# A list scheduler's cost table is replaced: a two-layer hybrid decoder on one Trainium2 core

## The chip, the cores and the metric

The kernel runs on one core of a Trainium2 chip. Its engines are TensorE (PE, matmuls into PSUM; PEld is its loading of stationary operands), VectorE (DVE), ScalarE (ACT), GpSimd (POOL) and SyncE (SP), which here only issues loads. Each engine takes its own list of instructions in order and waits on semaphores for the others. The metric is the device time of the core in microseconds (us), from three runs and one profiled execution.

## What is computed

Two layers. Each has a half-step SwiGLU FFN, then one block in which a Mamba-2 SSD mixer and a latent-attention (MLA) mixer run side by side on the same normalised input, and then a second half-step FFN. 256 positions, model width 1024, FFN width 2816, 32 SSD heads of 64 in 4 groups with state 128, 8 attention heads, all in float32.

```python
for l in range(DEPTH):                                  # DEPTH = 2
    h = h + 0.5 * swiglu(rms_norm(h, ln_ffn1[l]), ffn1_w13[l], ffn1_w2[l])
    u = rms_norm(h, ln_mix[l])
    z, xbc, dt_raw, cq, ckv, kr, gates = split_cols(u @ w_in[l], IN_SPLIT_SIZES)
    y_ssd = ssd_branch(z, xbc, dt_raw, ...)             # conv, silu, chunked scan, norm, w_out
    y_mla = mla_branch(cq, ckv, kr, cos, sin, ...)      # q/k/v up, norms, rope, causal softmax, w_out
    g = sigmoid(gates)
    h = h + (g[..., :D_MODEL] * y_ssd + g[..., D_MODEL:] * y_mla) @ w_o[l]
    h = h + 0.5 * swiglu(rms_norm(h, ln_ffn2[l]), ffn2_w13[l], ffn2_w2[l])
```

## The kernel before

**Arithmetic.** Every large matrix product is made from split operands. A weight block of 128 x 1024 float32 is loaded by SP into a staging buffer `st` (four of them); ACT rounds it to `wh` (fp32r), DVE subtracts to get the rest, `wl` (four buffers each, `ahead`). The activations are split likewise: `X`, `oT` and `A` hold a high half of 256 columns and a low half of 256 columns (`operand`: ACT writes the high half, DVE the low one). In the FFNs, the gates and the SSD output, `mm2` makes one matmul of `wh` on both halves (512 columns) and one of `wl` on the high half (256 columns) for each 128 rows. Elsewhere `mm` makes three matmuls of 256 columns. The smaller products of the scan and of attention are in float32; the scan's output matmuls (`s<-dec,xdt`) write 64 of the 128 output rows each and come in pairs, the "narrow" form.

**Stages.** `run` goes through FFN 1, `mix`, FFN 2 for each layer. `mix` begins with the latent projections, then on DVE a chain of small steps: softplus of the time steps (tile `kn`), the latent norms (`lm`, `rly`, `rlt`, `Rc`, `Rf`), `dt`, `dA`; a small matmul on `dA` gives the cumulative sums `acum`, which go through DRAM as `rows` and come back broadcast by POOL as `row`. Then `loop_order` interleaves convolutions (`bc`, `xs`), queries, keys and values, eight `ssd` steps, eight attention `head` steps and the `z` gates. In a convolution (`conv_pair`) ACT starts `cy` and DVE adds three taps one after the other into the same tile. In `ssd`, PE transposes `xs`, DVE multiplies into `xdt`, ACT makes the decays `dec`, DVE masks them, and PE multiplies. In `head`, PE transposes queries and keys, ACT writes `qkT`, PE makes scores, DVE takes maxima, ACT exponentiates into `pp`, PE transposes that, ACT copies it to `pT`, PE makes the output. After the loop come the gates, the output projections and FFN 2.

**The order.** No engine call in the program goes to the hardware as it is written. `Queue` hands each to `Order.add`, which records it as a `Step` with its operands, works out which earlier steps it needs, and prices it with `Order.cost`: `pitch` is how long it holds its engine, `tail` what passes after that until another engine may use the result (a negative `tail` marks a load of that many bytes). `Order.arrange` then plays the program through once with these prices and writes down the order in which each engine takes its steps; `emit` issues all of them in that order, from one line (L335), so that every instruction in the profile carries it and tiles tell them apart. In `arrange`, an engine that is free looks at the first 12 (`LOOK`) of its waiting steps in program order and takes the first whose operands and buffers are ready at that time of the plan; PE wants results of other engines to be `MARGIN` older than that. SP looks only at its first step, and so keeps program order. In the plan, a result is ready for a step on the same engine after `pitch`, for another engine after `pitch + tail`. The plan's times steer nothing once the order is written: on the chip, each engine waits for what it really needs.

Of the kernel before, what the change touches and what calls it, by code (L numbers as in the profile page):

```python
# [17 lines left out]
AF = mybir.ActivationFunctionType  # L18
ALU = mybir.AluOpType

P = 128
# [16 lines left out]
XSB, ZB = 2, 1  # L38
STBUF = 4
GB, SB, HB = 4, 2, 2  # L40
LOOK, MARGIN = 12, 250.0


V_LN1, V_LNM, V_LN2 = 0, 8, 16
# [107 lines left out]


class Step:
    __slots__ = ("engine", "call", "args", "kw", "tiles", "pitch", "tail", "index", "needs", "then", "ready", "far", "at")


class Queue:
# [7 lines left out]
class Order:  # L166


    TAIL = {"PE": 190.0, "ACT": 140.0, "DVE": 120.0, "POOL": 200.0, "SP": 0.0}

    def __init__(self, nc):
        self.steps = []
        self.tensor, self.scalar = Queue(self, "PE", nc.tensor), Queue(self, "ACT", nc.scalar)
# [3 lines left out]
    @staticmethod  # L177
    def cost(engine, name, args, kw):

        views = [v for v in (*args, *kw.values()) if isinstance(v, View)]  # L180
        out = kw.get("out", args[0] if args else None)
        if name == "dma_start":
            return (600.0 if engine == "POOL" else 470.0), 4.0 * max(v.arr.size for v in views)
        size = lambda v: v.arr.size // v.shape[0]
        if engine == "PE":
            if name == "transpose":
                return 109.0, 0
            n, dt = size(kw["rhs"]), kw["lhsT"].tile.what[1]
            if dt == F32R:
                return n / 2.4 + 13.5, 0  # L190
            if dt == BF16:
                return n / 2.4 + 4.0, 0
            pair = 0.55 if out.shape[0] < P else 1.0
            return max(2 * (n / 1.2 + 2.5), 60.0) * pair, 0
        n = max(size(v) for v in views)
        if engine == "ACT":
            t = 85.0 + 0.845 * n
            if name == "activation":
                t += 45.0 * sum(isinstance(kw.get(k), View) for k in ("scale", "bias"))
                t += 235.0 * ("accum_out" in kw)  # L200
            return t, 0
        t = 66.0 + 1.042 * n
        if name == "scalar_tensor_tensor":
            t += 60.0
        return t, 0

    def add(self, engine, name, call, args, kw):
        s = Step()
        s.engine, s.call, s.args, s.kw, s.index = engine, call, args, kw, len(self.steps)
        s.pitch, size = self.cost(engine, name, args, kw)  # L210
        s.tail = self.TAIL[engine]
        if size:
            s.tail = -size
        outs = [kw["out"]] if "out" in kw else [args[0]]
        ins = [*args[0 if "out" in kw else 1:], *(v for k, v in kw.items() if k not in ("out", "accum_out"))]
        if "accum_out" in kw:
            outs.append(kw["accum_out"])
        outs = [v for v in outs if isinstance(v, View)]
        ins = [v for v in ins if isinstance(v, View)]
        before = set()  # L220
        meet = lambda a, b: a[0] < b[1] and b[0] < a[1] and a[2] < b[3] and b[2] < a[3]
        within = lambda a, b: b[0] <= a[0] and a[1] <= b[1] and b[2] <= a[2] and a[3] <= b[3]
        for v in ins:
            before.update(o for o, g in v.tile.writes if meet(g, v.region))
        for v in outs:
            t = v.tile
            before.update(o for o, g in t.writes if meet(g, v.region))
            before.update(o for o, g in t.reads if meet(g, v.region))
        for v in outs:
            t = v.tile  # L230
            t.writes = [(o, g) for o, g in t.writes if not within(g, v.region)]
            t.reads = [(o, g) for o, g in t.reads if not within(g, v.region)]
            t.writes.append((s, v.region))
        for v in ins:
            v.tile.reads.append((s, v.region))
        s.tiles = list({id(v.tile): v.tile for v in (*outs, *ins)}.values())
        for t in s.tiles:
            t.left += 1
        s.needs, s.then, s.ready, s.far, s.at = len(before), [], 0.0, 0.0, None
        for o in before:  # L240
            o.then.append(s)
        self.steps.append(s)

    def arrange(self):

        engines = ("PE", "ACT", "DVE", "POOL", "SP")
        free = dict.fromkeys(engines, 0.0)
        waiting = {e: [] for e in engines}
        wire, done = 0.0, 0
        events = []  # L250
        wake = lambda t, e: heapq.heappush(events, (t, engines.index(e)))
        for s in self.steps:
# [19 lines left out]
        while events:  # L272
            now, e = heapq.heappop(events)
# [23 lines left out]
            s = pick  # L297
            waiting[e].remove((s.index, s))
            s.at = now
            free[e] = now + s.pitch  # L300
            if s.tail < 0:
                wire = max(wire, now + 1300.0) + -s.tail / 380.0
                end = wire + (2500.0 if e == "POOL" else 700.0)
            else:
                end = now + s.pitch + s.tail
            done += 1
            wake(free[e], e)
            for t in s.tiles:
# [8 lines left out]
                    for x in engines:  # L317
                        wake(t.free_at, x)
            for n in s.then:
                near = n.engine == e and s.tail >= 0  # L320
                n.ready = max(n.ready, now + s.pitch if near else end)
                if not near:
                    n.far = max(n.far, end)
                n.needs -= 1
                if not n.needs:
                    heapq.heappush(waiting[n.engine], (n.index, n))
# [856 lines left out]
```

## Time and profile before

| | us |
|---|---|
| median of 3 runs | 1478.0 (1471.64 to 1480.55) |
| profiled execution, its own time | 1476.14 |
| its span, first to last instruction | 1474.4 |
| PE busy in the span | 1449.2 (98%) |
| DVE busy | 1148.3 (78%) |
| ACT busy | 928.4 (63%) |

The kernel's stages in the span: FFN 1 of the first layer to about 205 us, its mixer to 567, FFN 2 to 750, FFN 1 of the second layer to 932, its mixer to 1292, FFN 2 to the end. Busy time of an engine is the union of its instructions' durations; matmuls are pipelined and their ends are modelled, so how many matmuls start in a stretch says more of PE's speed than its busy time. The granted clock (PEclk) is a share of TensorE's full 2.4 GHz. A wait is idle time of an engine, put down to the instruction that ended it.

### The profile page before, as it was taken

What the parts mean: (1) busy time and instruction counts of PE and PEld (TensorE: products, weight loads), DVE (VectorE), ACT (ScalarE), POOL (GpSimd) and SP (SyncE); (2) the same over time, 40 slices, a digit from 0 to 9 for tenths busy, and PEclk for the clock granted to TensorE, in tenths of its full rate; (3) what the DMA queues carried; (4) which work ended last, traced back from release to release, by engine and by line L of the source; (5) the groups of instructions that cost most, each with busy time, mean ns of one, the idle gap of its engine ahead of it and who ended that gap; (6) DMA issues with size and microseconds to landing.
All of it is one profiled execution on the core that took longest, in us unless ns stands there. A gap on an engine that the chain in (4) does not pass through costs nothing.

```text
span 1474.4 us, 25056 instructions
## 1 busy us (share of the span) xinstructions
PE 1449.2 (98%) x9418; PEld 1309.6 (89%) x9418; DVE 1148.3 (78%) x2081; ACT 928.4 (63%) x1754; POOL 18.6 (1%) x38
## 2 busy tenths in 40 slices
PE   7999999999999999999999999989999999999999
PEld 6888898999888998888888888989999889988888
DVE  7877679889977668787677876898889676788864
ACT  6555457998875456555455554688898554565542
POOL 0000000000000000000000000000000000000000
PEclk9999999999999999999999999999999999999999
DMA  6655655455545555556655566555454455555563
GB/s 234 195 183 183 186 177 174 150 163 162 167 134 183 185 183 181 191 191 179 194 189 190 192 179 196 168 161 169 157 166 155 157 182 185 184 183 191 191 194 110
DMA packets 75978, 261.43 MB, mean 177 GB/s; under 512 B 8880, under 2 KB 11184, under 8 KB 75856
## 3 DMA queue, kind: packets, MB, share of 16 engines
q1 hardware_dynamic: 73232, 251.37, 53.1%
q0 software_dynamic: 2624, 8.46, 1.9%
q8 instruction: 74, 1.21, 0.3%
q14 instruction: 48, 0.39, 0.1%
HBM read 258.68 MB, written 1.11 MB: 176 GB/s over the span
## 4 chain that ended last, share of the span: by engine, by line
PE 81%; DVE 11%; ACT 5%; issue 2%; DMA 0%; SPq 0%; DVEq 0%; ACTq 0%
PE g L335 77%; DVE wl L335 4%; PE h L335 2%; PE s L335 2%; ACT dec L335 2%; DVE cy L335 2%; DVE dec L335 1%; ACT wh L335 1%; ACT pp L335 1%; DVE kn L335 0%; ACT A L335 0%; ACT cy L335 0%; DVE rqt L335 0%; DMA st<-in_w_dram 0%; DVE qp L335 0%
## 5 line engine op out<-in xcount | busy, mean ns | idle before, releaser
L335 DVE TENSOR_TENSOR wl<-st,wh 128x1024 fp32r<-128x1024 f32 (+2 forms) x488 | 580.7, 1192 | 239.1 <-ACT wh L335 234.8
L335 ACT CAST wh<-st 128x1024 fp32r<-128x1024 f32 (+2 forms) x488 | 499.3, 1025 | 410.3 <-PE g L335 313.7
L335 PE MATMUL g<-X,wh 128*128 128x256 f32 (+1 forms) x2464 | 617.7, 329 | 9.1 <-DVE X L335 7.0
L335 PE MATMUL g<-X,wl 128*128 128x256 f32 x1696 | 482.4, 285 | 0.0
L335 PEld LDWEIGHTS g<-X,wh 128*128 128x128 f32 x2464 | 417.8, 191 | 52.5 <-DVE X L335 7.5
L335 PE MATMUL g<-oT,wh 128*128 128x512 f32 (+1 forms) x1248 | 343.8, 344 | 0.0
L335 PE MATMUL g<-A,wh 128*128 128x512 f32 (+1 forms) x982 | 336.9, 389 | 0.0
L335 PEld LDWEIGHTS g<-X,wl 128*128 128x128 f32 x1696 | 324.7, 191 | 1.4 <-DVE wl L335 0.2
L335 PE MATMUL g<-oT,wl 128*128 128x256 f32 x976 | 274.4, 281 | 0.0
L335 PE MATMUL g<-A,wl 128*128 128x256 f32 x960 | 269.3, 281 | 0.0
L335 PEld LDWEIGHTS g<-oT,wh 128*128 128x128 f32 x1248 | 216.1, 189 | 29.6
L335 PEld LDWEIGHTS g<-A,wh 128*128 128x128 f32 x982 | 182.7, 188 | 40.0
L335 PEld LDWEIGHTS g<-oT,wl 128*128 128x128 f32 x976 | 184.9, 189 | 0.0
L335 PEld LDWEIGHTS g<-A,wl 128*128 128x128 f32 x960 | 181.5, 189 | 0.0
L335 DVE TENSOR_TENSOR t<-t,g 128x256 f32<-128x256 f32 x180 | 74.7, 415 | 0.5 <-ACT t L335 0.5
L335 DVE SCALAR_TENSOR_TENSOR cy<-g,vec,cy 128x255 f32<-128x255 f32 x144 | 68.9, 480 | 6.8 <-ACT cy L335 2.7
L335 ACT CAST A<-ta 128x256 fp32r<-128x256 f32 x88 | 35.5, 404 | 48.3 <-DVE ta L335 48.0
L335 ACT COPY t<-g 128x256 f32<-128x256 f32 x180 | 65.1, 362 | 0.3 <-PE g L335 0.3
L335 DVE TENSOR_TENSOR t<-t,Rb 128x512 f32<-128x512 f32 x88 | 60.9, 692 | 3.0
L335 PE MATMUL g<-wh,A 128*128 128x384 f32 (+1 forms) x192 | 55.4, 357 | 0.0
L335 ACT ACTIVATE dec<-row,acum 128x256 f32<-128x256 f32 (+1 forms) x128 | 49.7, 446 | 2.0 <-PE s L335 2.0
L335 ACT ACTIVATE ta<-t 128x256 f32<-128x256 f32 x88 | 36.5, 414 | 15.2 <-DVE t L335 15.1
(228 smaller groups left out, 1117.2 us busy)
## 6 DMA issues: line engine op xcount, KB each, us to landing
st<-in_w_dram SPq DMA_DIRECT2D x238, 512.0 KB, 4.2
st<-in_win_dram SPq DMA_DIRECT2D x124, 512.0 KB, 4.0
st<-in_wso_dram SPq DMA_DIRECT2D x32, 512.0 KB, 3.8
st<-in_w_dram SPq DMA_DIRECT2D x32, 384.0 KB, 3.1
row<-rows POOLq DMA_DIRECT2D x32, 256.0 KB, 3.9
st<-in_wmo_dram SPq DMA_DIRECT2D x16, 512.0 KB, 3.5
st<-in_wo_dram SPq DMA_DIRECT2D x16, 512.0 KB, 3.5
st<-in_wuq_dram SPq DMA_DIRECT2D x16, 384.0 KB, 3.6
```

Source lines behind the costliest of these rows:

```text
L335: s.call(*(take(v) for v in s.args), **{k: take(v) for k, v in s.kw.items()})
```

## The change

`Order.cost` gets a new table, and `arrange` treats some cases of their own. For ACT and DVE `tail` is now the time from a step's start to its result; `pitch` is shorter, and a dependent step on the same engine has to wait for the result too, not only for the engine (PE's own steps still follow each other after `pitch`). Prices differ by PSUM or SBUF source, by operation and by per-partition scalars. Narrow matmuls cost a switch of 95 ns in and out, functions of another activation table cost 1283 ns, PE is taken as 1.84 times slower in its first 7.5 us, the first load lands later, and `MARGIN` falls from 250 to 60 ns. 35 ns (55 ns for PE) are added to each result. No engine call of the program itself is changed.

```diff
-LOOK, MARGIN = 12, 250.0
+LOOK, MARGIN = 12, 60.0
@@ class Order
-    TAIL = {"PE": 190.0, "ACT": 140.0, "DVE": 120.0, "POOL": 200.0, "SP": 0.0}
@@ def cost
         if name == "dma_start":
-            return (600.0 if engine == "POOL" else 470.0), 4.0 * max(v.arr.size for v in views)
-        size = lambda v: v.arr.size // v.shape[0]
+            return (600.0 if engine == "POOL" else 450.0), 4.0 * max(v.arr.size for v in views)
         if engine == "PE":
             if name == "transpose":
-                return 109.0, 0
+                return 109.0, 270.0
             n, dt = size(kw["rhs"]), kw["lhsT"].tile.what[1]
             if dt == F32R:
-                return n / 2.4 + 13.5, 0
+                t = n / 2.4 + (17.0 if n > 256 else 11.0)
+                return t, t + 165.0
             if dt == BF16:
-                return n / 2.4 + 4.0, 0
-            pair = 0.55 if out.shape[0] < P else 1.0
-            return max(2 * (n / 1.2 + 2.5), 60.0) * pair, 0
+                return n / 2.4 + 4.0, n / 2.4 + 169.0
+            t = max(2 * (n / 1.2 + 2.0), 130.0)
+            if out.shape[0] < P and n > 1:
+                t = t * 0.5 + 40.0
+            return t, t + 165.0
         n = max(size(v) for v in views)
+        bank = any(v.tile.ring.bank for v in ins)
+        scalars = sum(isinstance(kw.get(k), View) for k in ("scale", "bias", "scalar", "scalar1"))
         if engine == "ACT":
-            t = 85.0 + 0.845 * n
-            if name == "activation":
-                t += 45.0 * sum(isinstance(kw.get(k), View) for k in ("scale", "bias"))
-                t += 235.0 * ("accum_out" in kw)
-            return t, 0
-        t = 66.0 + 1.042 * n
-        if name == "scalar_tensor_tensor":
-            t += 60.0
-        return t, 0
+            t = (160.0 + 0.8 * n if bank else 200.0 + 0.83 * n) + 100.0 * scalars
+            if "accum_out" in kw:
+                return t + 5.0, t + 240.0
+            return t - 100.0, t
+        slow = bank or name not in ("tensor_scalar", "tensor_copy", "memset")
+        t = 150.0 + (1.05 if slow else 0.56) * n + 60.0 * (scalars and name == "scalar_tensor_tensor")
+        return t - 83.0, t
@@ def add
-        s.tail = self.TAIL[engine]
-        if size:
-            s.tail = -size
+        s.load = name == "dma_start"
+        s.table = {AF.Silu: 1, AF.Exp: 2, AF.Tanh: 2, AF.Sin: 3}.get(kw.get("func"))
@@ def arrange
-        wire, done = 0.0, 0
+        wire, done, first, form, table = 2000.0, 0, None, False, 0
...
-            free[e] = now + s.pitch
-            if s.tail < 0:
-                wire = max(wire, now + 1300.0) + -s.tail / 380.0
-                end = wire + (2500.0 if e == "POOL" else 700.0)
-            else:
-                end = now + s.pitch + s.tail
+            pitch, tail = s.pitch, s.tail
+            if s.load:
+                wire = max(wire, now + 1300.0) + tail / 360.0
+                tail = wire + (2500.0 if e == "POOL" else 800.0) - now
+            elif e == "PE":
+                if first is None:
+                    first = now
+                if now < first + 7500.0:
+                    pitch *= 1.84
+                    tail += pitch - s.pitch
+                narrow = s.args[0].shape[0] == 64
+                if narrow != form:
+                    pitch, tail, form = pitch + 95.0, tail + 95.0, narrow
+            elif s.table and s.table != table:
+                pitch, tail, table = pitch + 1283.0, tail + 1283.0, s.table
+            free[e] = now + pitch
+            end = now + tail + 35.0
...
             for n in s.then:
-                near = n.engine == e and s.tail >= 0
-                n.ready = max(n.ready, now + s.pitch if near else end)
-                if not near:
-                    n.far = max(n.far, end)
+                if n.engine == e == "PE":
+                    n.ready = max(n.ready, free[e])
+                else:
+                    n.ready = max(n.ready, end + 20.0 * (n.engine == "PE"))
+                    n.far = max(n.far, n.ready)
```

## Rows read from the trace of the kernel before

**Rows 1.** The page's part 1: busy us, share of the span, instructions.

```profile
PE 1449.2 (98%) x9418; PEld 1309.6 (89%) x9418; DVE 1148.3 (78%) x2081; ACT 928.4 (63%) x1754; POOL 18.6 (1%) x38
```

**Rows 2.** Windows: length, busy of PE, PEld, DVE, ACT, POOL; PEclk, DMA share, GB/s.

```profile
0.00:23.00 23.00, 14.22 (x55) 11.43 (x55) 15.27 (x42) 14.36 (x28) 0.20 (x4) 0.87 0.78 261
...
205.00:430.00 225.00, 218.94 (x1667) 205.30 (x1667) 199.12 (x436) 187.86 (x428) 9.25 (x17) 0.99 0.49 158
932.00:1156.00 224.00, 217.69 (x1668) 203.86 (x1667) 197.93 (x427) 187.60 (x427) 9.13 (x17) 1.00 0.49 158
430.00:567.00 137.00, 136.80 (x920) 125.53 (x919) 95.96 (x165) 69.84 (x104) 0.00 (x0) 1.00 0.56 181
...
1292.00:1474.00 182.00, 178.83 (x1053) 158.48 (x1053) 127.56 (x190) 92.26 (x151) 0.00 (x0) 1.00 0.55 174
```

**Rows 3.** Waits of PE: total us, times, longest us.

```profile
PE g L335 <- DVE X L335: 7.0, 2, 6.7
PE s L335 <- DVE xdt L335: 4.4, 6, 1.2
PE s L335 <- DVE dth L335: 3.9, 2, 2.1
PE g L335 <- ACT wh L335: 1.8, 2, 1.0
PE h L335 <- ACT qkT L335: 1.2, 2, 0.9
PE s L335 <- DVE acum L335: 1.1, 2, 0.7
PE s L335 <- DVE BC L335: 0.8, 1, 0.8
```

**Rows 4.** Timeline of DVE, 232 to 238 us: start, duration, instruction, count.

```profile
232.60 0.55 DVE L335 RECIPROCAL kn<-kn 128x64 f32<-128x64 f32 x1
...
236.06 0.23 DVE L335 TENSOR_TENSOR Rc<-rly,rhy 128x2 f32<-128x2 f32 x2
236.33 0.16 DVE L335 TENSOR_TENSOR Rf<-Rc 128x4 f32<-128x4 f32 x1
236.53 0.17 DVE L335 TENSOR_SCALAR Rf<-Rf 128x4 f32<-128x4 f32 x1
...
236.75 1.51 DVE L335 SCALAR_TENSOR_TENSOR kn<-kn 128x64 f32<-128x64 f32 x6
```

**Rows 5.** Timeline of PE at 239 us, idle time before it in brackets.

```profile
239.03 0.83 PE L335 MATMUL s<-dA,cb 128*128 128x32 f32 x6 [2.09 <-DVE dth L335]
```

**Rows 6.** Timeline of DVE and PE, 304 to 312 us.

```profile
304.38 0.75 DVE L335 TENSOR_TENSOR xdt<-s,dth 128x256 f32<-128x256 f32 x2
...
304.86 1.52 PE L335 MATMUL s<-dec,xdt 128*64 128x256 f32 x16 [0.69 <-DVE xdt L335]
...
311.78 1.52 DVE L335 SCALAR_TENSOR_TENSOR cy<-g,vec,cy 128x255 f32<-128x255 f32 x3
```

**Rows 7.** Windows behind the first layer's stall at 239 us.

```profile
242.10:245.40 3.30, 3.30 (x18) 3.30 (x17) 2.96 (x13) 1.85 (x4) 0.13 (x1) 0.51 0.68 215
246.00:249.30 3.30, 3.30 (x30) 3.30 (x29) 3.17 (x6) 2.95 (x6) 0.72 (x2) 1.00 0.62 195
```

**Rows 8.** Windows of 150 us inside the first two FFN stages.

```profile
30.00:180.00 150.00, 150.00 (x851) 130.15 (x850) 117.92 (x201) 84.77 (x149) 0.00 (x0) 1.00 0.60 188
570.00:720.00 150.00, 150.00 (x867) 132.29 (x866) 115.94 (x178) 87.49 (x151) 0.00 (x0) 1.00 0.60 188
```

**Rows 9.** Windows in the start.

```profile
14.00:17.00 3.00, 1.21 (x6) 0.55 (x4) 2.86 (x11) 2.75 (x6) 0.00 (x0) 0.98 0.86 295
17.00:20.00 3.00, 3.00 (x11) 2.74 (x12) 2.52 (x8) 2.25 (x3) 0.00 (x0) 0.50 0.60 203
```

**Rows 10.** Groups of ACT by tile: count, busy us, mean ns, idle before.

```profile
L335 ACT ACT_TABLE_LOAD x6 | 7.7, 1283 | 0.8 <-PEq L1174 0.7
...
L335 ACT ACTIVATE sin<-ta 128x64 f32<-128x64 f32 x1 | 0.3, 256 | 0.0
```

More of the change, by code (lines that the diff above doesn't have):

```diff
@@ L154 @@
 class Step:
-    __slots__ = ("engine", "call", "args", "kw", "tiles", "pitch", "tail", "index", "needs", "then", "ready", "far", "at")
+    __slots__ = ("engine", "call", "args", "kw", "tiles", "pitch", "tail", "load", "table", "index", "needs", "then", "ready",
+                 "far", "at")
 class Queue:
@@ L181, in cost @@
         out = kw.get("out", args[0] if args else None)
+        ins = [v for v in views if v is not out]
+        size = lambda v: v.arr.size // v.shape[0]
         if name == "dma_start":
-            return (600.0 if engine == "POOL" else 470.0), 4.0 * max(v.arr.size for v in views)
-        size = lambda v: v.arr.size // v.shape[0]
+            return (600.0 if engine == "POOL" else 450.0), 4.0 * max(v.arr.size for v in views)
         if engine == "PE":
             if name == "transpose":
-                return 109.0, 0
+                return 109.0, 270.0
             n, dt = size(kw["rhs"]), kw["lhsT"].tile.what[1]
             if dt == F32R:
-                return n / 2.4 + 13.5, 0
+                t = n / 2.4 + (17.0 if n > 256 else 11.0)
+                return t, t + 165.0
             if dt == BF16:
-                return n / 2.4 + 4.0, 0
-            pair = 0.55 if out.shape[0] < P else 1.0
-            return max(2 * (n / 1.2 + 2.5), 60.0) * pair, 0
+                return n / 2.4 + 4.0, n / 2.4 + 169.0
[3 more added lines that the diff above has]
+            return t, t + 165.0
         n = max(size(v) for v in views)
+        bank = any(v.tile.ring.bank for v in ins)
+        scalars = sum(isinstance(kw.get(k), View) for k in ("scale", "bias", "scalar", "scalar1"))
         if engine == "ACT":
-            t = 85.0 + 0.845 * n
-            if name == "activation":
-                t += 45.0 * sum(isinstance(kw.get(k), View) for k in ("scale", "bias"))
-                t += 235.0 * ("accum_out" in kw)
-            return t, 0
-        t = 66.0 + 1.042 * n
-        if name == "scalar_tensor_tensor":
-            t += 60.0
-        return t, 0
+            t = (160.0 + 0.8 * n if bank else 200.0 + 0.83 * n) + 100.0 * scalars
[5 more added lines that the diff above has]
+        return t - 83.0, t
     def add(self, engine, name, call, args, kw):
@@ L209, in add @@
         s.engine, s.call, s.args, s.kw, s.index = engine, call, args, kw, len(self.steps)
-        s.pitch, size = self.cost(engine, name, args, kw)
-        s.tail = self.TAIL[engine]
-        if size:
-            s.tail = -size
+        s.pitch, s.tail = self.cost(engine, name, args, kw)
+        s.load = name == "dma_start"
+        s.table = {AF.Silu: 1, AF.Exp: 2, AF.Tanh: 2, AF.Sin: 3}.get(kw.get("func"))
         outs = [kw["out"]] if "out" in kw else [args[0]]
```

## The prediction

> **What bounds the kernel now.** The times are read first, then the page's busy shares, then the windows by stage, then what TensorE (PE) waits for, and last the timeline around each wait. The profiled execution took 1476.14 us: 1474.4 us of span and 1.74 us around it. The median of the three runs shown is 1478.0 us, 1.9 us above this execution, and they spread from 1471.6 to 1480.6. The sum below is made against 1476.1.
>
> PE is busy for 98% of the span, VectorE (DVE) for 78%, ScalarE (ACT) for 63% [rows 1]. So what an order of instructions can win is PE's idle time, its slow-clock time and what its rhythm loses, and no more. The windows say where the idle time lies [rows 2]: 8.8 us in the first 23 us, 6.1 us and 6.3 us in the two stretches where the SSD and attention steps interleave (205 to 430 and 932 to 1156), 0.2 us in the gate and output stretch, and 3.2 us in the last FFN with its tail. Only the two interleaved stretches have two engines close to full: DVE 199 of 225 us, ACT 188 of 225 us. An order that serves DVE badly would be felt there and nowhere else.
>
> The list of PE's waits names the releasers [rows 3]. The 7.0 us on the first `X` is the lead-in, which has nothing before it to reorder. `wh` (1.8 us) is also in the start. What is left is `xdt` 4.4, `dth` 3.9, `qkT` 1.2, `acum` 1.1, `BC` 0.8: 11.4 us, all but `qkT` behind DVE.
>
> **Why those waits are there.** PE obeys a list that a plan wrote; it stalls where the plan thought an operand would be done earlier than it was. The DVE timeline around 236 us shows what the plan has wrong [rows 4]. Two independent operations of 2 elements (`Rc` x2) take 0.23 us together, each about 0.16, so they start some 0.07 us apart. Two dependent ones (`Rf`, then `Rf`) start 0.20 us apart, and six dependent `kn` steps of 64 elements take 1.51 us, 0.25 us each. The old table lets a dependent DVE operation follow after its pitch: 66 + 1.042 x 4 = 70 ns for `Rf` against 200 measured, 66 + 67 + 60 = 193 ns for a `kn` step against 250. The new table makes it 150 + 4 + 35 = 189 ns and 150 + 67 + 35 = 252 ns. The old plan loses about 0.12 us per dependent plain operation and 0.06 per dependent scalar_tensor_tensor. The chain of softplus, latent rsqrt, `dt` and `dA` has some 11 of the first kind and 14 of the second, and a reciprocal of 0.55 us priced at 0.13: 11 x 0.12 + 14 x 0.06 + 0.4 = 2.6 us late (an estimate from these rows). PE's matmul on `dA` then stands idle 2.09 us [rows 5]: the lag less the 0.25 us that the old MARGIN held in reserve, and some slack. Row and mechanism agree in size.
>
> `xdt` is the same on a smaller scale [rows 6]: PE stands 0.69 us before the narrow matmuls. What runs on DVE in every convolution are three chained `cy` steps, here 1.52 us, 0.51 each, where the old table has 66 + 266 + 60 = 392 ns and the new 150 + 268 + 60 + 35 = 513.
>
> **The change, part by part.** No instruction is added or removed: the same ones are written in another order, and every term is a stall that moves. SP takes its steps in program order before and after, so the loads keep their order; each waits for a staging buffer that a `wl` conversion frees, and four buffers with a DMA share of 0.49 [rows 2] cover a conversion that comes a microsecond later. POOL carries only the `row` loads and `rows` stores, and nothing is moved past them.
>
> The Trainium skill speaks against this reading (VectorE: DVE Perf Modes, section "The DRAIN you can't avoid"): there the next DVE operation cannot start until the pipe of the one before has emptied, so chaining or not chaining would make no difference. The pair `Rc` x2 in 0.23 us, with 0.16 for one, says otherwise here, so I go by the row [rows 4]. By the rule, the gains of (1) to (4) below would be nothing and the time 1476 us.
>
> (1) Dependent DVE and ACT steps follow later in the plan, so `dA` and `acum` are planned for when they are ready. PE's 3.9 + 1.1 = 5.0 us [rows 3] can go only if other matmuls are in reach; the convolutions and the first query block are, if their weights are converted in time, and DVE can now convert weights in the gaps of the chain. I take 4.0 of 5.0: the reciprocal in the chain is still priced like any other operation, and PE to DVE to PE for `acum` remains. Bounds 0 and 5.0.
>
> (2) Behind the 2.09 us stall of the first layer the granted clock is 0.51 from 242.1 to 245.4, that is the 1.2 GHz level, and 18 matmuls fit where 30 fit at full clock [rows 7]: 3.3 x (1 - 18/30) = 1.3 us. In the second layer, after 1.8 us of the 3.9, the whole stretch shows 1.00 [rows 2]. I take -1.3 as following (1). Bounds 0 and 1.3.
>
> (3) `xdt`: 4.4 us in 6 waits. -3.0, because DVE is nearly full there and something else may come late instead. Bounds 0 and 4.4.
>
> (4) `BC` and `qkT`, 2.0 us: -1.0. Bounds 0 and 2.0.
>
> (5) MARGIN falls from 250 to 60 ns. Take a DVE result of 256 elements for PE, as `xdt`. Old: 66 + 267 + 120 + 250 = 703 ns after its start PE may be planned; new: 150 + 269 + 35 + 20 + 60 = 534. In the trace PE started 0.48 us after `xdt` did [rows 6]. The reserve falls from 0.22 to 0.05 us, 0.17 us less per handoff. Each layer has 8 x 3 such handoffs in the SSD steps, 8 x 4 in the heads and 4 in `bc`: 60, so 120 in all. If each cost the whole 0.17 us, that is +20 us; if the better table makes reserve needless, nothing. I take +1.5, near the lower end, because the new table meets the DVE rows compared above within some 10 ns. Behind a matmul that waits stands all of PE's list.
>
> (6) Each of the four FFN stages holds 528 pairs of a 512 and a 256 wide matmul, 1056 in all, and waits for nothing, but they don't all run at one rhythm [rows 8]: 851 matmuls in 150 us of the first, 867 in the same length of each of the other three (one row stands). That is 176.3 against 173.0 ns each, 3.4 us for a stage. Nothing in the waits explains it: PE shows no idle time in either stretch. It looks like a rhythm that a stage keeps once it has it. Another order before a stage may change it. Bounds: -3.4 (the first stage turns fast) to +10.2 (the other three turn slow). I take 0.
>
> (7) The start. PE is idle 1.8 us of the stretch 14 to 17 and then runs at clock 0.50 from 17 on [rows 9]. By the 0.87 of the first 23 us, it spends 0.13 / 0.5 x 23 = 6.0 us at the low level and loses 3.0 us. The DMA queues are 0.86 busy there, the loads keep their order, and neither the later first landing nor the 1.84 factor in the table changes what ACT has to do first. I take 0; bounds -4.8 and +2 (one more wait like the present two).
>
> (8) Priced but without effect: table loads at 1283 ns are what the rows show, six of them; but `sin` runs in 0.26 us with no load before it [rows 10], so the new plan sees one or two loads too many around 43 us, in a stage where ACT is busy 85 of 150 us [rows 8]. If that cover were gone it would cost 2.6 us. Narrow matmuls: eight of them take 1.52 us (16 records) [rows 6]; old table 4 x 237 + 4 x 120 = 1.43, new 4 x 255 + 4 x 149 = 1.62, 8 times in a layer; PE's real time does not change.
>
> Sum: -4.0 - 1.3 - 3.0 - 1.0 + 1.5 = -7.8. 1474.4 - 7.8 + 1.7 = 1468 us.
>
> **Rivals.** *Nothing gained*: the named stalls go and others of the same size take their place, since DVE at 199 of 225 us is not faster. For it: `xdt` waits come once in each period, behind a nearly full DVE; against it: the 2.1 us wait of `dA` has work that could stand before it. Of its chance, 0.02 is for the mechanism that a DVE operation starts alike whether it depends on the one before or not, so that no gap is there to fill; the `Rc` pair in [rows 4] is against it. That is the rule of the Trainium skill quoted above (same page and section). The time is 1476 us.
>
> *Thin reserve* (slower): term (5) at its upper end, in the 120 handoffs of the interleaved stretches. For it: the waits above exist even with 250 ns. Against it: they come from lag, which the table removes. 1476.1 - 9.3 + 20.3 = 1487 us; it decides from 55 handoffs on that wait 0.17 us each (9.3 / 0.17).
>
> *Chain cut open* (slower): DVE's plan sees a gap behind each dependent step and fills it with a weight conversion, about 1.1 us against the 0.12 it fills. With four `wl` buffers, at the softplus and rsqrt chain of each layer `dA` would come 4 x 1.0 = 4 us later: +8 us where I have -4.0, 1476.1 + 8.2 = 1484 us. Against it: the conversions must be done at some time, and PE needs them to have work.
>
> *All of it*: (1) to (4) in full, the first FFN fast, the start's two waits gone with (5) at nothing: -5.0 - 1.3 - 4.4 - 2.0 - 3.4 - 1.8 = -17.9, 1458 us.
>
> **How the numbers follow.** My forecast 0.45 (1461 to 1475), nothing gained 0.22, thin reserve 0.12, chain cut open 0.06, all of it 0.15. The time is the likeliest's, 1468. The range 1456 to 1486 leaves out about half of thin reserve and a third of all of it, and a little at the edges: under 2 in 10. It covers both signs; the likeliest's own is 1461 to 1475. One per cent is about what a measurement here can tell from no change: faster means under 1463.2, against the median of 1478.0. All of it and a sixth of my forecast: 0.22. Slower means over 1492.8: half of thin reserve and a little of chain cut open: 0.09. Within: 0.69.
>
> **What would show it.** In the waits of PE after: `dth` and `acum` under 1.5 us together, `xdt` under 2, no stretch at 0.5 around 242 us; in the DVE timeline the rsqrt and `kn` steps interleaved, some 0.1 us apart, with `wl` between. Thin reserve would show as many short PE waits on `qkT`, `pp`, `pT`, `dec`. Chain cut open would show `wl` between the `kn` steps and a `dth` wait above 3 us. The forecast is wrong if PE's idle time in the two stretches stays near 6 us each, or if windows of the FFN stages show fewer than 860 matmuls in 150 us where they now show 867.

## The result and the profile after

The new kernel takes 1454.12 us (1453.09 to 1457.06, 4 runs) beside 1478.17 for the kernel before: ratio 0.9847, 95% interval 0.9813 to 0.9882, 1.5% faster. Its profiled execution took 1457.06 us, with a span of 1455.3, against 1476.14 and 1474.4. The forecast was 1468 with a range from 1456 to 1486: the direction was right, the gain was more than twice as large as forecast (24 us where the medians were to differ by 10, 19.1 between the profiles where the sum had 7.8), and the time lies 1.9 us under the range.

Part 1 of the page after (it answers [rows 1]), and windows after ([rows 2, 8]; columns as there):

```profile
PE 1442.0 (99%) x9418; PEld 1305.5 (90%) x9418; DVE 1134.7 (78%) x2081; ACT 922.4 (63%) x1754; POOL 18.5 (1%) x38
```

```profile
0.00:23.00 23.00, 14.90 (x72) 12.28 (x73) 16.90 (x41) 15.80 (x31) 0.20 (x4) 1.00 0.79 277
...
205.00:430.00 225.00, 224.71 (x1707) 210.58 (x1706) 197.56 (x442) 190.48 (x436) 9.23 (x17) 1.00 0.51 163
...
932.00:1156.00 224.00, 223.63 (x1674) 208.17 (x1673) 196.32 (x427) 189.53 (x435) 9.11 (x17) 1.00 0.52 164
...
30.00:180.00 150.00, 149.20 (x845) 129.22 (x844) 116.00 (x196) 86.15 (x151) 0.00 (x0) 1.00 0.58 183
570.00:720.00 150.00, 150.00 (x867) 132.29 (x866) 113.91 (x174) 84.63 (x145) 0.00 (x0) 1.00 0.60 189
```

PE's idle time in the interleaved stretches fell from 6.1 and 6.3 us to 0.3 and 0.4. The counts of matmuls in these two windows (1707 after, 1667 before) say less: the windows stand at fixed times and hold another part of the program when a stage begins earlier, and the order of the kernel before alone gave 1667 and 1651 in two profiles. The granted clock is 1.00 in all these windows. The first FFN is still in the slow rhythm. PE's waits after (all of them; compare [rows 3]):

```profile
PE g L349 <- DVE X L349: 6.8, 1, 6.8
PE g L349 <- DVE t L349: 0.8, 1, 0.8
PE g L349 <- DVE wl L349: 0.8, 1, 0.8
PE g L349 <- ACT wh L349: 0.5, 1, 0.5
PE s L349 <- DVE dA L349: 0.4, 2, 0.2
```

The DVE timeline after, in the chain of [rows 4]:

```profile
229.24 0.18 DVE L349 TENSOR_SCALAR kn<-kn 128x64 f32<-128x64 f32 x1
229.80 1.22 DVE L349 TENSOR_TENSOR wl<-st,wh 128x1024 fp32r<-128x1024 f32 x1 [0.37 <-ACT wh L349]
...
231.48 1.21 DVE L349 TENSOR_TENSOR wl<-st,wh 128x1024 fp32r<-128x1024 f32 x1
...
233.81 0.15 DVE L349 SCALAR_TENSOR_TENSOR rlt<-rlt,lm 128x4 f32<-128x4 f32 x1
233.88 0.22 DVE L349 SCALAR_TENSOR_TENSOR kn<-kn 128x64 f32<-128x64 f32 x1
234.02 0.15 DVE L349 SCALAR_TENSOR_TENSOR rlt<-rlt 128x4 f32<-128x4 f32 x1
234.09 0.28 DVE L349 TENSOR_TENSOR qp<-qp,rob 128x128 f32<-128x128 f32 x1
...
237.76 0.23 DVE L349 SCALAR_TENSOR_TENSOR dA<-dt,expA 128x64 f32<-128x64 f32 x1
```

The rsqrt steps still follow each other after 0.2 us, but a softplus step (`kn`) or a piece of the query (`qp`) now starts between them, 0.07 to 0.14 us after the last start. Weight conversions stand in the chain too.

**Where the gain lies.** Every kernel without extra matmuls has the same 9418 matmul records, so the start of the k-th record can be compared. The table gives, for each kernel, by how many us a stretch is shorter than in the profile of the kernel before. `start` is records 0 to 1250 (start, FFN 1 and the first 19 us of the mixer), `mix 0` 1250 to 3500, `FFNs` 3500 to 5750, `mix 1` 5750 to 8250, `end` the rest. In the kernel before these edges lie at 223.9, 544.0, 926.7 and 1276.2 us, and in every kernel of the table the same matmuls lie between them.

```
                                          start  mix 0  FFNs  mix 1  end    sum
the kernel before, profiled again          6.2    0.0   0.0    0.0   0.0    6.2
the new kernel                             2.4    8.7   0.6    7.1   0.3   19.1
  again                                    2.5    7.8   0.5    7.3   0.3   18.5
  a third time                             6.0    7.8   0.5    6.8   0.3   21.5
new table, MARGIN 250                      2.0    9.4  -2.7    8.6   0.4   17.8
  again                                    2.2    9.6  -2.7    8.6   0.4   18.1
new table, no follow rule                  2.6   -0.8  -1.0   -2.8  -0.5   -2.5
new table, no reserve at all               6.5    5.6   0.0    3.4   0.0   15.4
old table, follow rule                     5.8    7.8   0.7    5.4   0.4   20.1
  on DVE alone                             6.5    6.3   0.7    5.3   0.4   19.2
  on ACT alone                             2.8    2.1  -3.5    1.7   0.0    3.1
  half the delay                           7.1    7.8   0.7    6.4   0.4   22.4
  double the delay                         6.5    7.2   0.7    5.5   0.4   20.3
  DVE, up to 64 elements                   5.1    6.3   0.7    4.6   0.4   17.2
  DVE, above 64 elements                   5.6    0.1   0.0   -0.4  -3.3    2.2
  known to the plan, not woven             3.2    4.9   0.7    4.6   0.4   13.8
  a twentieth of the delay                 2.1    4.0  -3.5    2.3   0.0    4.9
old table, MARGIN 60                       2.0   -1.3  -3.7   -2.0  -0.1   -5.0
```

Of the new kernel's 19.1 us the two mixers hold 15.8, the start 2.4 and the edges between stages 0.9. The first line says that the start's part can't be claimed for the change: the same kernel profiled twice differs by 6.2 us there, and by nothing afterwards.

### The profile page after: what moved, and what is told of

Its sections match the earlier page's. It is cut to its first block, busy times and chain, and to the rows that moved or that the text cites. A ratio compares the mean times of both kernels' runs of the same rounds, so it can differ in the third digit from the quotient of the medians.

```text
span 1455.3 us, 25054 instructions
## 1 busy us (share of the span) xinstructions
PE 1442.0 (99%) x9418; PEld 1305.5 (90%) x9418; DVE 1134.7 (78%) x2081; ACT 922.4 (63%) x1754; POOL 18.5 (1%) x38
## 4 chain that ended last, share of the span: by engine, by line
PE 54%; issue 41%; ACT 2%; DMA 2%; DVE 1%; SPq 0%; POOL 0%; ACTq 0%; DVEq 0%; POOLq 0%
PE g L349 49%; PE h L349 3%; PE s L349 2%; DMA st<-in_w_dram 1%; ACT wh L349 1%; DVE wl L349 0%; DMA row<-rows 0%; DMA rows<-pp 0%; DMA hT<-in_x_dram 0%; ACT kn L349 0%; ACT dec L349 0%; ACT pp L349 0%; ACT qkT L349 0%; DVE A L349 0%; DVE kn L349 0%
## 5 line engine op out<-in xcount | busy, mean ns | idle before, releaser
L349 DVE SCALAR_TENSOR_TENSOR cy<-g,vec,cy 128x255 f32<-128x255 f32 (+1 forms) x144 | 67.9, 477 | 4.4 <-ACT cy L349 2.9
```

The costliest lines, as they stand in the source:

```text
L349: s.call(*(take(v) for v in s.args), **{k: take(v) for k, v in s.kw.items()})
```

## Experiments

### What in the change does it: the follow rule, or MARGIN

Four kernels undo or do one part. The follow rule is the one by which a DVE or ACT step waits in the plan for the result of its own engine.

`e1_follow`, the old table with the rule alone:

```diff
-                near = n.engine == e and s.tail >= 0
+                near = n.engine == e == "PE"
```

> The old table and the old MARGIN of 250, with one line changed: a DVE or ACT step that depends on one of its own engine waits in the plan for the result (pitch + 120 or + 140 ns) instead of the pitch alone. Lag theory (the stalls come from dependent steps that the plan lets follow too early): the waits on dth, acum and xdt fall from 9.4 us in all to under 2.5, the mixer stages give back 10 to 15.5 of the 15.5 us that they gave with the whole change, the time is 1462 to 1467 us. Reserve theory (MARGIN is what mattered): within 3 us of the kernel before, waits on xdt stay near 4 us. Prices theory (only the whole table does it): between the two, 3 to 8 us.

`e2_margin`, the old table with the smaller reserve alone:

```diff
-LOOK, MARGIN = 12, 250.0
+LOOK, MARGIN = 12, 60.0
```

> The old table with MARGIN 60 in place of 250, nothing else. Lag theory: the stalls grow, because the lag is not covered any more: each of some 10 waits by up to 0.19 us and new ones among the 120 handoffs, 2 to 20 us slower than before (1478 to 1498), with waits on xdt above 4.4 us. Reserve theory: 5 to 15 us faster than before. Prices theory: within 3 us of before.

`e3_nofollow`, the new kernel without the rule:

```diff
-                if n.engine == e == "PE":
+                if n.engine == e and not s.load:
```

> The new kernel with one line taken back: a DVE or ACT step may follow one of its own engine after the pitch, as in the old plan; prices, MARGIN 60 and the rest stay new. Lag theory: waits on dth, acum and xdt come back and are longer than before (the reserve is gone): 9 to 25 us in all, 1467 to 1485 us. Reserve or prices theory: within 4 us of the new kernel, 1453 to 1459 us.

`e4_m250`, the new kernel with `MARGIN` 250:

> The new kernel with MARGIN 250 in place of 60. Lag theory: the table has removed the waits, so the reserve is worth little either way: within 3 us of the new kernel, waits of PE outside the start under 2 us. Reserve theory: most of the gain is lost, 1465 us or more.

Measured on one chip, where the kernel before took 1473.63 us: e1 1455.53 (0.9874, 0.9846 to 0.9902), e2 1480.06 (1.0046, 1.0027 to 1.0066), e3 1479.03 (1.0036, 1.0020 to 1.0051), e4 1454.52 (0.9877, 0.9853 to 0.9901). In time, the one line gives as much as the whole change. By stage it does not: its mixers gave 13.2 us, those of the new table at the same `MARGIN` (e4) 18.0, and in e4's profile a slow FFN stage took 3.4 us back (`FFNs`, -2.7 against 0.7). Waits of PE in e1 (all of them):

```profile
PE g L335 <- DVE X L335: 7.1, 2, 6.6
PE h L335 <- ACT keT L335: 1.8, 1, 1.8
PE h L335 <- ACT qkT L335: 1.4, 1, 1.4
PE g L335 <- ACT wh L335: 1.4, 1, 1.4
PE g L335 <- DVE wl L335: 0.8, 1, 0.8
```

Those on `dth`, `acum` and `xdt` are gone. The 3.2 us on ACT's `keT` and `qkT` stand in the mixers; e4 has no such wait, and they are most of what the rest of the table adds. Without the rule nothing is gained: e3 is slower than the kernel before, and by only 1.0 us faster than e2, which has the old prices at the same `MARGIN`; the two intervals overlap. The new prices without the rule at `MARGIN` 250 were not run. Waits of PE in e2, then in e3:

```profile
PE s L335 <- DVE xdt L335: 5.8, 6, 1.6
PE s L335 <- DVE dth L335: 3.5, 2, 1.8
PE h L335 <- ACT pp L335: 2.3, 8, 0.3
```

```profile
PE s L349 <- DVE dth L349: 6.2, 2, 3.2
PE s L349 <- DVE xs L349: 2.4, 4, 0.6
PE s L349 <- DVE xdt L349: 2.4, 5, 0.7
```

With the old table the smaller reserve shows as the forecast's rival had it, short waits on `pp` and longer ones on `xdt`, though with 6 us and not the rival's 20. e1 came out better than the lag theory's own range of 1462 to 1467.

### How much is chance of the run

`e5_before_again` and `e6_after_again` are the two kernels unchanged.

> The kernel before, unchanged, profiled a second time. Two terms of the change's ledger stand outside the mixer: the start gave 2.4 us (no stretch at clock 0.50 behind 17 us), and the first FFN's slow rhythm (851 matmuls in 150 us). If the order of instructions sets them: again 0.50 from 17 to 23 us, 851 matmuls in 30:180, and again the stretch at half clock behind the mixer's stall at 239 us. If they hang on the moment at which the run falls: at least one of the three is different. In both cases the waits on dth, acum and xdt are the same as before within 0.5 us, since they come from the order.

> The new kernel, unchanged, profiled a second time. If the order sets the rhythm: 30:180 again shows about 851 matmuls and the time is within 1 us of 1457. If it hangs on the moment: it may show 867 and a time near 1453.5, which is what two of its four timed runs gave. Waits of PE outside the start under 1.5 us either way.

e5 took 1469.92 us, e6 1457.65, one execution each. The waits on `dth`, `acum` and `xdt` in e5 are 3.9, 1.1 and 4.4, to the tenth those of [rows 3]. Three other things moved: the start stays at full clock, the first FFN runs in the fast rhythm, and the stretch at half clock behind the first mixer's stall lies elsewhere, with a second one in the second mixer, where the profile before has none. Windows of e5, then the second mixer's stretch in the profile before, where the same work stands 6.2 us later:

```profile
17.00:20.00 3.00, 2.72 (x17) 2.20 (x16) 2.72 (x12) 1.77 (x2) 0.00 (x0) 1.00 0.54 182
30.00:180.00 150.00, 150.00 (x868) 131.16 (x867) 118.70 (x201) 85.99 (x148) 0.00 (x0) 1.00 0.62 192
...
234.00:237.40 3.40, 3.08 (x14) 2.69 (x15) 3.26 (x14) 2.43 (x7) 0.63 (x1) 0.51 0.53 165
...
961.10:964.50 3.40, 3.30 (x16) 3.10 (x15) 3.16 (x14) 2.89 (x7) 0.51 (x1) 0.50 0.51 169
```

```profile
967.30:970.70 3.40, 3.25 (x28) 3.13 (x27) 3.16 (x14) 2.90 (x7) 0.51 (x1) 1.00 0.52 168
```

So the start and the first FFN's rhythm can differ with the same order (of the new kernel, e6 shows the slow rhythm again and the third profile the fast one). In the mixers, e5 and the profile before agree within 0.05 us, e6 and the new kernel within 0.9. The half clock in e5's second mixer puts PE 1.4 us behind by record 6125, and by record 6200 it is level again, since a wait of 0.8 us on `BC` and other idle time are gone there: lost clock and waits do not simply add up.

### The rhythm of an FFN stage

`e7_kick` disturbs the first FFN of the new kernel. The expectation counts eight extra matmuls; the edit makes nine.

```diff
+            if l == 0 and which == 1 and i > 4 and i % 2:
+                nc.tensor.matmul(self.sps()[:, :1], lhsT=self.all, rhs=gu[:, 0, :1], start=True, stop=True)
```

> The new kernel with eight extra one-column float32 matmuls in the first FFN of layer 0, one after each second block pair from the sixth on; their results are not read. Each costs PE at most 0.25 us, 2 us in all. Theory that a stage keeps the rhythm it entered with until it is disturbed: between the kicks the pairs of a 512 and a 256 wide matmul keep one rhythm each, 346.7 or 353.3 ns, and at least one kick changes it; the time is within +2 and -2 us of the new kernel's. Rival, that something in this stage (its loads, the DVE and ACT work beside it) makes it slow: 353.3 ns returns after every kick, and the time is 2 us longer.

It took 1456.68 us in its one execution. The mean of a pair, from the starts of its matmuls, before the first kick and after each of the nine, in ns:

```
353.3 | 353.3  346.7  346.7  353.3  346.7  346.7  353.3  346.7  346.7 (to the end of the stage)
```

Each stretch keeps one value until the next kick, and both values come back in the same stage with the same loads beside it: the rhythm is a state that a disturbance draws anew, six fast of nine here. In later stages it came out alike whenever an order was profiled again: `e4_m250` and its repetition below show the slow one in FFN 2 both times.

### DVE, ACT, and the length of the delay

`e8_dve` and `e9_act` give the rule to one engine:

```diff
-                near = n.engine == e and s.tail >= 0
+                near = n.engine == e and s.tail >= 0 and e != "DVE"     # e9: e != "ACT"
```

> The old table and MARGIN 250; only dependent DVE steps wait in the plan for the result, dependent ACT steps follow after the pitch as before. If DVE's chains are the cause, as all waits but qkT say: at least four fifths of what the rule for both engines gave, 1456 to 1462 us against 1474 before on this chip's runs, waits on xdt, dth and acum under 2.5 us together, that on qkT unchanged at 1 to 1.5 us. If ACT's chains matter as much (softmax, decays): half of the gain or less, 1463 us or more.

> The old table and MARGIN 250; only dependent ACT steps wait in the plan for the result, dependent DVE steps follow after the pitch. With DVE alone the waits on xdt, dth and acum went and the time fell by 15 us. If ACT's chains add nothing of their own: the waits of the kernel before within 1.5 us, 9.4 us on xdt, dth and acum together, and a gain behind 223 us of under 3 us. If the two are alternatives (either one spaces the plan enough): waits under 4 us.

e8: 1457.21 us beside 1473.58 (0.9897, 0.9881 to 0.9914), with no wait left on `xdt`, `dth` or `acum`, and against the expectation none on `qkT` either; e9, one execution: 1472.99 beside 1474.53, with waits on `xdt` 4.2, `dth` 4.0, `acum` 1.1, as before. DVE's chains carry it: 11.6 us of the mixers' gain with DVE alone, 13.2 with both. (e9's FFN stages fell into the slow rhythm; its mixers gave 3.8.)

`e10_half` and `e11_double` change the delay:

```diff
-                n.ready = max(n.ready, now + s.pitch if near else end)
+                n.ready = max(n.ready, now + s.pitch + 0.5 * s.tail * (e != "PE") if near else end)   # e11: 2.0
```

> The old table and MARGIN 250; dependent DVE and ACT steps follow in the plan after pitch + 60 and + 70 ns, half of the delay of e1_follow. Lag theory: the lag of a chain halves, a chain of 25 steps is late by some 1 us instead of 2.6, and the reserve of 0.25 us covers a part: waits on dth, acum and xdt of 2 to 5 us in all, 1459 to 1466 us where the full delay gives 1455.5 and none 1474. Threshold theory (any gap makes the plan weave independent steps between, and that is enough): as with the full delay, 1454 to 1458, waits under 1.5 us.

> The old table and MARGIN 250; dependent DVE and ACT steps follow after pitch + 240 and + 280 ns, twice the delay of e1_follow and some 120 ns more than the chip needs. Lag theory: too long a delay costs only idle time that the plan sees and fills; no wait of PE comes back, DVE's chains stretch; 1455 to 1461 us. Rival, chain cut open: each gap takes a weight conversion of 1.1 us, the chains end late in truth and PE waits behind them, over 1465 us with waits on dth or acum above 3 us.

1454.6 us (0.9858, 0.9834 to 0.9882) and 1457.91 (0.9879, 0.9855 to 0.9903) beside 1474.53. Half is as good as the whole, as the threshold theory had it and the lag theory in its plain form had not; double costs little.

### Knowing the delay, or weaving through it

`e15_hold` lets the plan know the delay, but an engine that meets such a step holds for it as the old plan's sequence did. `e16_tiny` has a delay of 6 or 7 ns, too short to make the plan's chains right but enough to make the engine take another step. The edit of e15, without the lines that set `near` up:

```diff
+                if now < s.near and at <= s.near:
+                    later = s.near
+                    break
...
-                n.ready = max(n.ready, now + s.pitch if near else end)
+                if near and e != "PE":
+                    n.near = max(n.near, end)
+                n.ready = max(n.ready, now + s.pitch if near and e == "PE" else end)
```

The first three lines let the engine hold when only a result of its own is missing. The edit of e16:

```diff
-                n.ready = max(n.ready, now + s.pitch if near else end)
+                n.ready = max(n.ready, now + s.pitch + 0.05 * s.tail * (e != "PE") if near else end)
```

> The old table and MARGIN 250; the plan knows that dependent DVE and ACT steps have to wait for the result, as in e1_follow, but the engine holds for such a step instead of taking another one meanwhile: an honest plan of the old, unwoven sequence. If it is the plan's honesty that counts (PE's matmuls are put where the operand is really there): waits of PE on dth, acum and xdt under 2.5 us in all and at least two thirds of the gain, 1455 to 1462 us. If it is the weaving (DVE's chains become shorter in truth): waits stay small because the plan knows them, but DVE fills up, PE gets idle time elsewhere, and less than half of the gain is there, 1466 us or more.

> The old table and MARGIN 250; dependent DVE and ACT steps follow after pitch + 6 and + 7 ns, a twentieth of the delay of e1_follow. The plan is as wrong on a chain's length as the old one within 5 per cent, but at the moment the pitch ends the dependent step is not yet ready, so that another one is taken if there is one. Weaving theory: nearly the whole gain, 1455 to 1460 us. Honesty theory: nearly none, 1470 us or more.

e15: 1462.36 us (0.9912, 0.9890 to 0.9934), e16: 1464.04 (0.9950, 0.9933 to 0.9967), beside 1474.04. Neither theory alone: knowing gives 9.5 us in the mixers, weaving 6.3, the rule with both 12.7 to 14.2 in the old table (e1, e10, e11). The 6.3 are from one profile, of an execution that took 1471.47 where the fastest of ten took 1462.49; its time holds two slow FFN stages and a slow start besides. What knowing can't give is seen in e15's waits:

```profile
PE s L340 <- DVE dth L340: 3.6, 2, 1.8
PE s L340 <- DVE acum L340: 0.9, 2, 0.5
```

and in its DVE timeline, where the chain still runs alone:

```profile
233.02 1.78 DVE L340 SCALAR_TENSOR_TENSOR kn<-kn 128x64 f32<-128x64 f32 x7
```

The `xdt` waits are gone, since PE's matmuls are placed later; the stall at the mixer's start stays as it was, and the profile shows no other work of PE in it. In e16 the waits on `dth` are gone, and others have come on ACT's tiles, `qkT` 2.0 and `kn` 1.6.

### Which chains

`e13_short` and `e14_long` apply the rule to the followers of DVE steps of up to 64 and of more than 64 elements. The edit of e13 (e14 has `> 64`):

```diff
-                near = n.engine == e and s.tail >= 0
+                near = n.engine == e and s.tail >= 0 and not (e == "DVE" and max(v.arr.size // v.shape[0] for v in (*s.args, *s.kw.values()) if isinstance(v, View)) <= 64)
```

> The old table and MARGIN 250; among same-engine followers only those of DVE operations of up to 64 elements (the softplus, latent and query rsqrt chains) wait for the result. If the forecast's terms were split rightly: the mixer's start gives its 9 us (dth and acum waits under 1.5 us), xdt keeps half or more of its 4.4, the time is 1461 to 1466 us against 1474.5. If the short chains also make the xdt waits (a query rsqrt stands ahead of it): xdt too under 1.5 us, 1456 to 1459 us.

> As before, but only followers of DVE operations of more than 64 elements wait (convolution taps, gates, FFN products, activations' low halves). Forecast's split: dth and acum waits stay at 5 us, those on xdt and BC fall under 2 us, 1467 to 1471 us. If only the short chains matter: within 3 us of the kernel before.

e13: 1458.93 us (0.9899, 0.9884 to 0.9913); e14: 1474.3 (0.9997, 0.9983 to 1.0011), beside 1474.04. In e13 no wait on `xdt` is left. In e14 PE's waits are:

```profile
PE s L335 <- DVE dth L335: 3.6, 2, 1.8
PE g L335 <- DVE cy L335: 3.5, 6, 0.7
PE s L335 <- DVE acum L335: 1.1, 2, 0.7
PE s L335 <- DVE xdt L335: 1.0, 2, 0.5
```

The waits on `xdt` fell here too, from 4.4 to 1.0, but 3.5 us on `cy` came in their place: the stall moved, and the time stayed. The small operations carry the gain.

### The reserve

`e12_noreserve` takes all reserve out of the new kernel:

```diff
-LOOK, MARGIN = 12, 60.0
+LOOK, MARGIN = 12, 0.0
-            end = now + tail + 35.0
+            end = now + tail
-                    n.ready = max(n.ready, end + 20.0 * (n.engine == "PE"))
+                    n.ready = max(n.ready, end)
```

> The new kernel with every reserve taken out: MARGIN 0, and the 35 and 20 ns added to each result gone, so that PE is planned 115 ns closer behind DVE and ACT than in the new kernel and some 60 ns before the chip can follow. Lag theory: waits come to the 120 handoffs of the mixers, at most 0.06 us each, 2 to 8 us in all, 1456 to 1463 us, with short waits on many tiles. Rival, reserve is worth nothing once the table is right: within 2 us of the new kernel.

The 35 ns go from dependent steps of one engine and from the release of buffers too, so this is not the reserve of PE alone. 1467.91 us (1460.64 to 1471.45; 0.9945, 0.9925 to 0.9965) beside 1474.53: worse than expected. Its one profile is of an execution of 1461.49, where the mixers gave 9.0 us; its longest waits in the mixers are 0.9 us in all on `dA` and 0.9 on `xs`. Why other runs take up to 10 us more was not seen.

`e17_after` and `e18_m250` are the new kernel and `e4_m250` again, side by side.

> The new kernel unchanged, timed in more rounds on one chip beside its variant with the old reserve. Between two profiles of it the mixers' gain over the kernel before agreed within 0.7 us (15.8 and 15.1); its time is to lie 1.2 to 1.6 per cent under the kernel before.

> The new table with MARGIN 250 a second time, beside the new kernel on the same chip. In its first profile the mixers gave 18.1 us against 15.8 in the new kernel, and two later FFN stages lost 2.7 us to a slower rhythm. If the larger reserve is a gain of its own in the mixers: 17 to 19 us there again, and the time 1 to 4 us under the new kernel's where the FFN rhythms are alike. If that was chance: mixers within 1 us of the new kernel's 15 to 16, times within 1 us.

1454.32 us (0.9862, 0.9835 to 0.9889) and 1454.95 (0.9869, 0.9844 to 0.9894) beside 1473.52. In the mixers the larger reserve is worth some 3 us (18.2 against 14.6 to 15.8), and it was not chance. Windows of e18:

```profile
205.00:430.00 225.00, 225.00 (x1713) 211.17 (x1712) 199.50 (x442) 190.18 (x436) 9.22 (x17) 1.00 0.51 164
570.00:720.00 150.00, 150.00 (x851) 129.99 (x850) 112.05 (x170) 82.27 (x141) 0.00 (x0) 1.00 0.59 186
```

No idle time is left in the first mixer's stretch. But FFN 2 of the first layer runs at 851 in 150 us, the slow rhythm, where the new kernel has 867, and that takes 3.3 us back (`FFNs`, -2.7 against 0.6). The two versions tie; none that was run beats the new kernel beyond its measurement.

## Why the prediction fell short

*The mechanism* was right and is shown: dependent DVE steps that the plan let follow too early, in the chains of small operations. e1, e3 and e13 carry it. Independent operations start as the new table says (it holds DVE for 71 ns at 4 elements and 134 at 64; the timeline after has 0.07 us from `rlt` to `kn` and 0.14 from `kn` to `rlt`), and filling the gap between dependent ones works. The Trainium skill (VectorE: DVE Perf Modes, section "The DRAIN you can't avoid") has the next operation wait until the pipe of the one before is empty, and in the same section lets one that is not held start earlier; the prediction took the first half alone. The trace shows the second: `kn` starts 0.07 us behind `rlt`, which lasts 0.15. The weaving by itself gave 6.3 us in the mixers (e16).

*Steps (1) to (4), the sizes.* This is the step that failed. I had -5.3, -3.0 and -1.0, together -9.3, and -12.7 at most. With the reserve kept, the mixers gave -18.0 and -18.2 (e4, e18); with (5), -14.6 to -15.8 where the sum had -7.8. Two things failed in it. First, I took 4.0 of 5.0, 3.0 of 4.4 and 1.0 of 2.0, against the chance that a full DVE brings other stalls; only 0.4 us on `dA` came, and not even the `acum` round trip is left among the waits. The reason given for (3), a DVE that is not faster, was wrong as well: DVE is busy for 1134.7 us instead of 1148.3, since busy time is the union of the durations and woven operations overlap.

Second, I bounded the gain by 11.4 us in the list of PE's waits and 1.3 us of clock, 12.7 us. The windows that I had read said 6.1 and 6.3 of idle time, 1.0 more than the list; and some of what was won counts as busy time. PE's busy time for the same 9418 matmuls fell from 1449.2 to 1442.0; in the two profiles with neither a slow start nor a slow first FFN it fell from 1444.9 (e5) to 1439.3 (e17). That "no more" than idle time, clock and rhythm could be won was wrong. The Trainium skill warns of the measure (Trainium Kernel Development and Optimization, section "Performance Expectations"): matmul busy time is a bad measure of how near a kernel is to its limit, because matmuls are pipelined. The trace agrees, by some 4 us in the mixers here. From start to start of the matmuls, the two mixers of the kernel before hold 12.6 us of idle time and 657.0 us without it, those of e4 none and 651.5. Of these 5.5 us, 1.7 lie between fp32r matmuls, where the 1.3 us of half clock were; the rest is spread over the small float32 matmuls (the time up to the transposes of `pp` fell from 8.5 to 6.0 us, up to those of `qkT` from 6.7 to 5.2, and others rose). What lets these start sooner is not shown.

*Split of (1) and (3).* The waits on `xdt` do not come from a full DVE: e13 removes them with the short chains alone, and DVE is busy for 197.6 us of the first stretch after, where it was 199.1. That it is the query's rsqrt chain ahead of `xdt` is likely but not shown, since e13 changes all short chains at once.

*Step (5), the reserve.* +1.5 expected, about +3 measured (18.2 against 14.6 to 15.8). Sign and bounds were right. The reserve is not needless once the table is right: 115 ns less for PE than in the new kernel, with 35 less for the other dependent steps, costs over 10 us (e12, against 1454 to 1457).

*Steps (6) and (7).* I gave the start and the first FFN's rhythm to the order and set them at 0. They differ between executions of one order. The execution that the sum was made against had a slow start and a slow first FFN, 6.2 us above e5 by nothing but this, and a central value of 0 left out that another execution may have neither. Of the 19.1 us between the two profiles 2.4 lie there, of the 21.5 in the third profile 6.0. These terms, on top of the mixers, took the time out of the range: 1476.1 less 15.8 alone is 1460. Whether the new order also makes a good start likelier is open: the granted clock was 0.999 or 1.0 in all eleven executions of the new kernel and 0.994 to 0.998 in 61 of the 62 of the kernel before that were timed beside the experiments, and those have no trace that says where it was low. The rhythm as a state that a stage keeps is shown by e7, and that another order may flip a later stage by e4 and e18.

*Step (8)* held: six table loads again, and nothing of it in the waits.

*The rivals.* "Thin reserve" is, in sign, what happened with the old table (e2), and is a small loss beside the right one. "Chain cut open" did happen in its first half: conversions stand in the chain, and from the first `kn` step to `dA` it takes 8.5 us (229.24 to 237.76) where it took 6.3. PE did not wait for it beyond 0.4 us on `dA`, and with twice the delay (e11) no wait on `dth` or `acum` came either. That those conversions give PE its other matmuls was the argument against the rival; it fits, and e15 fits it from the other side, where the chain is let through alone and PE waits 1.8 us. "All of it" has the right time, 1458 for an execution that took 1457.06, and that is partly luck: it counted 3.4 us for a fast first FFN, which stayed slow there (845 in 150 us), and 12.7 for the mixers, which gave 15.8. The median of the timed runs, 1454.12, lies under the range, whose lower end had no room for a faster start on top of the mixers' gain.

## What to carry to other kernels

When a scheduler's plan is wrong, look for the chains of small dependent operations first: a fixed latency per step adds up there. Tell the scheduler the time until a result can be used on the same engine, not only how long the engine is held; half of it did as well here (e10), and a twentieth, which only makes the engine take other work meanwhile, gave 6.3 of some 13 us in the mixers (e16). Before a sum is made against one profiled execution, profile the same kernel twice: what differs between the two can't be claimed for a change. PE's idle time and its slow clock are not the whole of what an order can win: in e4 they were 13.9 of 18 us.

## What the runs showed of the hardware

A stream of alternating 512 and 256 wide matmuls has two steady rhythms, 346.7 and 353.3 ns a pair, with no idle time shown in either (e5 and the profile before, 30 to 180 us). The slow one is a cycle of three pairs of 349, 350 and 361 ns. A stage of 528 pairs kept its rhythm until something disturbed it (e7); the slow one costs 3.4 us a stage. On DVE, independent operations started before the one in front had ended (0.07 us apart where one lasts 0.16), dependent ones some 0.04 us after its end; a reciprocal of 64 elements took 0.55 us, where a tensor-tensor operation of that size takes 0.22.
